# Second feed-forward of a two-layer transformer kernel: up projections by Strassen's scheme, the down projection as a phase of its own

## The chip, the cores and the metric

The kernel runs on one core of a Trainium2 chip. The core has a matrix engine (TensorE, PE in the profile, with its weight loads listed apart as PEld), a vector engine (VectorE, DVE), a scalar engine (ScalarE, ACT), GpSimd (POOL) and a sync engine (SP). SP, ACT and POOL issue DMA transfers between memory (DRAM) and the on-chip memory (SBUF); PE writes its sums to PSUM, from where DVE and ACT read them. The metric is the device time of one execution in microseconds (us).

## The reference, cut to what matters

Two layers on 1024 tokens (and, in layer 0 only, 256 context tokens) of width 1024, all in 32-bit floats. Each layer has a mixer (layer 0 attention, layer 1 a gated linear attention, GLA) and a feed-forward part with a convolution over three tokens. The change concerns the feed-forward part of layer 1 and the final norm behind it.

```python
def conv_ffn(x, w_up, conv_w, conv_b, w_down):      # x: 1024 x 1024, w_up: 1024 x 5632, w_down: 2816 x 1024
    h = x @ w_up
    ch = h.shape[-1]
    h = lax.conv_general_dilated(h, conv_w[:, None, :], window_strides=(1,),
                                 padding=((1, 1),), feature_group_count=ch, ...) + conv_b
    u, gt = jnp.split(h, 2, axis=-1)
    return (jax.nn.silu(gt) * u) @ w_down
...
        h = h + g1 * y
        h = h + g2 * conv_ffn(rms_norm(h, norm2_g[layer]) * (1.0 + sc2) + sh2, ffn_w_up[layer],
                              ffn_conv_w[layer], ffn_conv_b[layer], ffn_w_down[layer])
...
    return rms_norm(h, final_norm_g)
```

## The kernel before

All activations lie transposed: h is eight tiles of 128 channels by 1024 tokens (h0 to h7 in the rows, as hh0 to hh7). A product of 32-bit floats is made of three matmuls: each operand is split into a high part, rounded to the type that PE multiplies (fp32r), and a low part, the rest, and wh·xh, wh·xl and wl·xh are added up in PSUM. `split` (L92 casts on ACT, L72 subtracts on DVE) makes the two parts. `load_w` brings 128 x 1024 weights (512 KB) on SP's queue into `wraw`, which has two buffers, and splits them into `whi` and `wlo`, three buffers each. `proj` (the matmuls of L109) runs one such tile against 1024 channels of the activation, 24 matmuls of 512 tokens. PSUM has two tiles `big` of three banks of 512 and two tiles `sm` of one.

The end of the kernel, in program order: `out_pass` twice (the output projection of GLA, first for tokens 0 to 511, then for 512 to 1023, tile names gA and gB), each of eight steps that add a projection to a row of h. In the second call the norm of tokens 0 to 511 (`norm_mod`, through `rstd_rows`) is made beside the projections after its step 1. `rstd_rows` squares the rows of h on ACT, adds them on DVE into `acc`, sums over channels with one matmul with ones (L127), and takes the inverse root as `yr` on ACT and DVE; `norm_mod` then makes `nu` (scaled rows) and x4h and x4l (the split operand), two DVE rows for each of eight channel blocks.

Then `ffn` runs for the 22 chunks c of 128 hidden channels. Each chunk has two parts, u (column block c of the up weights) and the gate (block c + 22): 48 matmuls of 512 tokens each into a `big`, then the convolution, one ACT row and two DVE rows (scalar_tensor_tensor of 1023, L69) straight from PSUM into `cv`. ACT's silu and one DVE product make the gated product, which is split into gh and gl. After every second chunk `down` runs the down projection of the two finished chunks: eight output blocks by two token halves, six matmuls each into an `sm` (L887), and DVE adds each into h. At the end the last three chunks are finished by token ranges (0 to 511, then 512 to 767 and 768 to 1023, matmuls of 256), and each finished range is normed by `final`, which stores the output by turns on SP's and ACT's queue.

PE's order is written out by hand (`manual_schedule`) from the second `out_pass` to the first projections of `ffn`; elsewhere a scheduler orders each engine's queue by priority and readiness, and the tiles' buffers decide what waits for what.

## Time and profile before

| | us |
|---|---|
| median of 3 runs (lowest to highest) | 3166.31 (3165.25 to 3168.08) |
| profiled execution, its own time | 3165.92 |
| its span, first to last instruction | 3164.1 |
| PE busy in the span | 3048.6 (96%) |
| DVE busy | 2026.3 (64%) |
| ACT busy | 1142.1 (36%) |
| POOL busy | 29.9 (1%) |
| mean granted TensorE clock | 0.987 |

The page gives each engine's busy time, the groups of instructions by line with the mean time of one, and what ended the idle time before them. Matmuls are pipelined: a matmul's recorded duration covers part of its neighbours', so how many fit in a stretch is read from the distance of their starts. The granted clock is a share of full speed (2.4 GHz); 0.5 is 1.2 GHz.

### The profile page before, as it was taken

To read this page: it belongs to the slowest core of one execution; us is meant where nothing else is said; L and a number is where in the kernel's file an instruction comes from. 1 tells how busy PE (TensorE), PEld (TensorE's weight loads), DVE (VectorE), ACT (ScalarE), POOL (GpSimd) and SP (SyncE) were. 2 spreads that over 40 slices of the span, in tenths; PEclk is the share of its full clock that TensorE was granted. 3 is DMA by queue.
4 is the path that set the end of the run, shared out by engine and by line. 5 is a ranking of instruction groups with operands and counts; after the bars stand their busy time and mean duration, and the time that the engine had idled before them with its cause. 6 is when DMAs were issued, how large, how long until landed. Compare 5 with 4: busy or idle time off the path is not lost. (4 is left out here: it accounts for less than half of the span.)

```text
span 3164.1 us, 40097 instructions
## 1 busy us (share of the span) xinstructions
PE 3048.6 (96%) x16390; PEld 2570.0 (81%) x16390; DVE 2026.3 (64%) x3124; ACT 1142.1 (36%) x1884; POOL 29.9 (1%) x50
## 2 busy tenths in 40 slices
PE   8788799999999999999999999999999999999998
PEld 4676689998878888888888788888877888888887
DVE  7667688886588555454455697668766554555446
ACT  5110277776342122122122365445444222222223
POOL 0000000000000000000000000000000000000000
PEclk9989899999999999999999999999999999999999
DMA  6665762212435111111111141110141111111111
GB/s 222 176 173 177 193 167 67 61 54 62 159 115 184 42 40 36 38 40 39 36 41 40 47 154 34 37 57 31 41 175 67 47 43 58 47 47 40 60 47 60
DMA packets 139184, 257.46 MB, mean 81 GB/s; under 512 B 22676, under 2 KB 82196, under 8 KB 139000
## 3 DMA queue, kind: packets, MB, share of 16 engines
q1 hardware_dynamic: 122168, 234.67, 22.7%
q0 software_dynamic: 15104, 18.13, 2.5%
q8 instruction: 129, 2.11, 0.3%
q10 hardware_dynamic: 1728, 2.10, 0.2%
q14 instruction: 55, 0.45, 0.0%
...
## 5 line engine op out<-in xcount | busy, mean ns | idle before, releaser
L92 ACT CAST whi<-wraw 128x1024 fp32r<-128x1024 f32 x218 | 226.2, 1048 | 1120.4 <-PE big L109 638.5
L72 DVE TENSOR_TENSOR wlo<-wraw,whi 128x1024 fp32r<-128x1024 f32 x218 | 264.4, 1221 | 483.0 <-ACT whi L92 481.4
L109 PE MATMUL big<-x2h,whi 128*128 128x512 f32 (+1 forms) x1056 | 377.5, 358 | 1.8 <-ACT crow L75 1.2
L109 PE MATMUL big<-x2l,whi 128*128 128x512 f32 (+1 forms) x1056 | 377.1, 357 | 0.4 <-DVE x2l L69 0.3
L109 PE MATMUL big<-x2h,wlo 128*128 128x512 f32 (+1 forms) x1056 | 377.2, 357 | 0.0
L887 PE MATMUL sm<-gh,whi 128*128 128x512 f32 (+1 forms) x904 | 332.6, 368 | 2.5 <-DVE h L69 1.4
L887 PE MATMUL sm<-gl,whi 128*128 128x512 f32 (+1 forms) x904 | 329.3, 364 | 0.2 <-DVE gl L72 0.2
L887 PE MATMUL sm<-gh,wlo 128*128 128x512 f32 (+1 forms) x904 | 328.7, 364 | 0.0
L69 DVE SCALAR_TENSOR_TENSOR cv<-big,cw,cv 128x1023 f32<-128x1023 f32 (+1 forms) x264 | 267.2, 1012 | 21.0 <-ACT cv L75 17.7
L109 PE MATMUL big<-x4l,whi 128*128 128x512 f32 x704 | 277.8, 395 | 0.9 <-DVE x4l L69 0.9
L109 PE MATMUL big<-x4h,whi 128*128 128x512 f32 x704 | 276.7, 393 | 1.9 <-ACT x4h L75 1.9
L109 PE MATMUL big<-x4h,wlo 128*128 128x512 f32 x704 | 274.0, 389 | 0.0
L69 DVE SCALAR_TENSOR_TENSOR h<-sm,G,h 128x512 f32<-128x512 f32 (+1 forms) x280 | 179.8, 656 | 90.6 <-PE sm L887 89.8
L109 PEld LDWEIGHTS big<-x2h,whi 128*128 128x128 f32 x1056 | 198.8, 188 | 34.1 <-ACT crow L75 2.0
L109 PEld LDWEIGHTS big<-x2l,whi 128*128 128x128 f32 x1056 | 198.8, 188 | 32.5 <-DVE x2l L69 1.1
L109 PEld LDWEIGHTS big<-x2h,wlo 128*128 128x128 f32 x1056 | 198.6, 188 | 31.1
L887 PEld LDWEIGHTS sm<-gh,whi 128*128 128x128 f32 x904 | 170.3, 188 | 41.1 <-DVE h L69 6.9
L69 DVE SCALAR_TENSOR_TENSOR hh<-sm,G,hh 128x512 f32<-128x512 f32 (+1 forms) x192 | 137.5, 726 | 87.5 <-PE sm L887 87.2
L887 PEld LDWEIGHTS sm<-gh,wlo 128*128 128x128 f32 x904 | 170.4, 188 | 27.6 <-issue 0.2
L887 PEld LDWEIGHTS sm<-gl,whi 128*128 128x128 f32 x904 | 170.4, 189 | 26.6 <-DVE gl L72 0.6
L75 ACT ACTIVATE cv<-big,cb,cw 128x1024 f32<-128x1024 f32 (+1 forms) x132 | 130.6, 990 | 125.0 <-DVE cv L69 124.5
L109 PEld LDWEIGHTS big<-x4h,whi 128*128 128x128 f32 x704 | 132.2, 188 | 34.1 <-ACT x4h L75 3.2
...
## 6 DMA issues: line engine op xcount, KB each, us to landing
mraw<-in_mod_wt_dram SPq DMA_DIRECT2D x88, 512.0 KB, 3.8
wraw<-in_ffn_up_dram SPq DMA_DIRECT2D x88, 512.0 KB, 3.2
wraw<-in_ffn_down_dram SPq DMA_DIRECT2D x44, 512.0 KB, 3.2
...
wraw<-in_attn_w_out_dram SPq DMA_DIRECT2D x16, 512.0 KB, 3.8
wraw<-in_gla_w_v_dram SPq DMA_DIRECT2D x16, 512.0 KB, 3.2
wraw<-in_gla_w_out_dram SPq DMA_DIRECT2D x16, 512.0 KB, 3.3
```

Of the source, the lines that this page charges most:

```text
L69: return self.nc.vector.scalar_tensor_tensor(out=out, in0=in0, scalar=scalar, in1=in1, op0=op0, op1=op1)
L72: return self.nc.vector.tensor_tensor(out=out, in0=a, in1=b, op=op)
L75: return self.nc.scalar.activation(out=out, in_=in_, func=func, **kw)
L92: self.nc.scalar.copy(hi, src)
L109: self.nc.tensor.matmul(ps[:, t0:t0 + n], a[:, k, :], b(k, t0, n), start=(k == 0 and j == 0), stop=(k == KD - 1 and j == 2))
L887: nc.tensor.matmul(o, w[:, d * P:(d + 1) * P], x[:, t0:t0 + n], start=(i == 0), stop=(i == 3 * len(group) - 1))
```

## The change

In layer 1 `ffn` is replaced. Layer 0 keeps it.

The up projections of a pair (u and the gate of chunk c) form one product of a 256 x 1024 and a 1024 x 1024 matrix. It is cut into 2 x 2 blocks: the weights into A11, A12, A21 and A22 (128 x 512 each, 1 for u, 2 for the gate, the second digit the half of the channels), the activation into B11, B12, B21 and B22 (512 channels by 512 tokens). Winograd's form of Strassen's scheme takes seven block products P1 to P7 instead of eight, each of 12 matmuls (four channel blocks by three parts): P1 = A11·B11, P2 = A12·B21, P3 = S4·B22, P4 = A22·T4, P5 = S1·T1, P6 = S2·T2, P7 = S3·T3. S1 to S4 are sums and differences of weight blocks, made on DVE for each pair; T1 to T4 are those of the activation, made once by `forms_last`, in place in h. Partial results are added on DVE from PSUM into rooms of 128 x 1024, from which the convolution now reads.

Since h's tiles serve as rooms, h goes to DRAM in both calls of `out_pass` (`spill`, on POOL's queue). Each gated product is stored to DRAM (`gs`, 512 KB, on POOL's queue). Behind the 22 pairs `down_pass` runs three times, for tokens 0 to 511, 512 to 767 and 768 to 1023. Each pass loads and splits all 22 down weights and the gated products of its tokens (`dx`), holds all eight output blocks in PSUM over the 22 chunks, and adds them into h once at its end. h is loaded back within the first pass, and the final norms of the first two ranges stand within the third. PE's order is written out by hand to the end.

In the whole kernel weights are now split in two halves of 512 (`split_half`, one set of 12 buffers of 512 for high and low parts).

```diff
     def load_w(self, src):
-        raw = self.wp.tile([P, 1024], F32, name="wraw", tag="wraw", bufs=2)
+        raw = self.raw_w()
         self.dma(raw, src)
-        hi = self.wp.tile([P, 1024], F32R, name="whi", tag="whi", bufs=3)
-        lo = self.wp.tile([P, 1024], F32R, name="wlo", tag="wlo", bufs=3)
-        self.split(hi, lo, raw, self.urgent)
+        return tuple(zip(*(self.split_half(raw[:, c:c + 512], self.urgent) for c in (0, 512))))
+
+    def raw_w(self):
+        return self.wp.tile([P, 1024], F32, name="wraw", tag="wraw", bufs=2)
+
+    def split_half(self, a, urgent=False):
+        hi, lo = (self.wp.tile([P, 512], F32R, name=n, tag="wf", bufs=12) for n in ("wh", "wl"))
+        self.split(hi, lo, a, urgent)
         return hi, lo
...
+                    if spill:
+                        self.dma2(self.h2[n][t0 // 512], h[n][:, t0:t0 + c])
...
+    def forms_last(self, h, X, A, B):
+
+        y = self.rstd_rows(lambda k, a, b: h[k][:, a:a + b], 512, 512)
+        k4 = range(4)
+        u11, u12, u21, u22 = ([h[k + j][:, t:t + 512] for k in k4] for j, t in ((0, 0), (0, 512), (4, 0), (4, 512)))
+        b1, b2 = ([B[:, k + j:k + j + 1] for k in k4] for j in (0, 4))
+        for k in k4:
+            self.stt(u12[k], u12[k], A[:, k:k + 1], y, ALU.mult, ALU.mult)
+            self.tt(u12[k], u12[k], u11[k], ALU.subtract)
+            self.split(*X["T1"][k], u12[k])
+        for k in k4:
+            hi, lo = X["B22"][k]
+            self.stt(u22[k], u22[k], A[:, k + 4:k + 5], y, ALU.mult, ALU.mult)
+            self.act(hi, u22[k], AF.Identity, bias=b2[k])
+            self.stt(lo, u22[k], b2[k], hi.bitcast(F32), ALU.add, ALU.subtract)
+        for k in k4:
+            self.stt(u22[k], u22[k], b2[k], u12[k], ALU.add, ALU.subtract)
+            self.split(*X["T2"][k], u22[k])
+        for k in k4:
+            self.stt(u11[k], u22[k], b1[k], u11[k], ALU.subtract, ALU.subtract)
+            self.split(*X["T3"][k], u11[k])
+        for k in k4:
+            self.stt(u21[k], u21[k], b2[k], u22[k], ALU.add, ALU.subtract)
+            self.split(*X["T4"][k], u21[k])
...
+    def pair_forms(self, l, c, w, fw, order):
+
+        rg = fw.tile([P, 1024], F32, name="graw", tag="graw", bufs=1)
+        self.dma(rg, self.io["ffn_up"][l, c + NFF])
+        ru = w["raw"]
+        S = {"A11": ru[:, :512], "A12": ru[:, 512:], "A21": rg[:, :512], "A22": rg[:, 512:]}
+
+        def get(n):
+            if n not in S:
+                x, y, op = {"S1": ("A21", "A22", ALU.add), "S2": ("S1", "A11", ALU.subtract), "S3": ("A11", "A21", ALU.subtract),
+                            "S4": ("A12", "S2", ALU.subtract)}[n]
+                x, y = get(x), get(y)
+                S[n] = fw.tile([P, 512], F32, name="S", tag="S", bufs=3)
+                self.tt(S[n], x, y, op)
+            return S[n]
+        for p in order:
+            w[p] = self.split_half(get({1: "A11", 2: "A12", 3: "S4", 4: "A22", 5: "S1", 6: "S2", 7: "S3"}[p]))
...
+            q.order = (5, 3, 6, 7, 4) if c < 2 else (1, 5, 6, 7, 2, 3, 4)
...
+        def prod(q, p):
+            if p == 1:
+                q.big, q.b = self.big(), self.sm()
+                q.a, q.cc, q.d = (q.big[:, 512 * i:512 * i + 512] for i in range(3))
+            ps, start = {1: (q.a, True), 2: (q.a, False), 5: (q.cc, True), 3: (q.cc, False), 6: (q.b, True), 7: (q.d, True), 4: (q.d, False)}[p]
+            (wh, wl), x = q.w[p], X[self.OPERAND[p]]
+            for k in range(4):
+                s = slice(k * P, (k + 1) * P)
+                for j, (a, b) in enumerate(((wh, x[k][0]), (wh, x[k][1]), (wl, x[k][0]))):
+                    nc.tensor.matmul(ps, a[:, s], b, start=(start and k == 0 and j == 0), stop=(k == 3 and j == 2), skip_group_check=True)
...
+            u, e = room[q.c % 2], q.c % 2
+            with self.tc.high_priority():
+                if p == 1:
+                    q.p1 = fw.tile([P, 512], F32, name="p1", tag="p1", bufs=2)
+                    nc.scalar.copy(q.p1, q.a)
+                elif p == 2:
+                    nc.scalar.copy(u[:, :512], q.a)
+                elif p == 5:
+                    q.p5 = half(5, e)
+                    nc.scalar.copy(q.p5, q.cc)
+                elif p == 6:
+                    q.u2 = half(6, e)
+                    self.tt(q.u2, q.b, q.p1, ALU.add)
+                    self.tt(q.p5, q.p5, q.u2, ALU.add)
+                elif p == 7:
+                    self.tt(room[2][:, 512:], q.d, q.p5, ALU.add)
+                elif p == 4:
+                    self.tt(room[2][:, :512], q.d, q.u2, ALU.add)
+                if p == 3:
+                    q.has12 = True
+                if q.u2 is not None and q.has12:
+                    self.tt(u[:, 512:], q.cc, q.u2, ALU.add)
+                    q.has12 = False
...
+        def end(q):
+            cv = []
+            for part, x in ((0, room[q.c % 2]), (1, room[2])):
+                j = q.c + NFF * part
+                y = room[3 + part]
+                cw = self.cw[:, j, :]
+                self.act(y, x, AF.Identity, scale=cw[:, 1:2], bias=self.cb[:, j:j + 1])
+                self.stt(y[:, 1:], x[:, :NM - 1], cw[:, 0:1], y[:, 1:], ALU.mult, ALU.add)
+                self.stt(y[:, :NM - 1], x[:, 1:], cw[:, 2:3], y[:, :NM - 1], ALU.mult, ALU.add)
+                cv.append(y)
+            self.last = self.act(cv[1], cv[1], AF.Silu)
+            self.tt(cv[0], cv[0], cv[1], ALU.mult)
+            self.dma2(self.gs[q.c], cv[0])
+
+        q = begin(0)
+        prod(q, 1)
+        done(q, 1)
+        prod(q, 2)
+        nxt = begin(1)
+        prod(nxt, 1)
+        done(nxt, 1)
+        prod(nxt, 2)
+        self.pair_forms(l, 0, q.w, fw, q.order)
+        last_forms()
+        done(q, 2)
+        for c in range(NFF):
+            for p in q.order:
+                prod(q, p)
+                done(q, p)
+            if c == 0:
+                self.pair_forms(l, 1, nxt.w, fw, nxt.order)
+                done(nxt, 2)
+            else:
+                nxt = begin(c + 1) if c + 1 < NFF else None
+            end(q)
+            q = nxt
...
+    def down_pass(self, l, h, t0, n, dp, mid={}):
+
+        nc = self.nc
+        g = self.G[l][1][:, :, 0]
+        per = 512 // n
+        tiles = [self.big() for _ in range(2 if n == 512 else 1)]
+        banks = [t[:, 512 * i:512 * i + 512] for t in tiles for i in range(3)]
+        banks += [self.sm() for _ in range(2 if n == 512 else 1)]
+        ps = [banks[d // per][:, n * (d % per):n * (d % per) + n] for d in range(KD)]
+        for c in range(NFF):
+            w = self.load_w(self.io["ffn_down"][l, c])
+            x = dp.tile([P, 512], F32, name="dx", tag="dx", bufs=4)[:, :n]
+            self.dma(x, self.gs[c][:, t0:t0 + n])
+            xh = dp.tile([P, 512], F32R, name="dh", tag="dh", bufs=4)[:, :n]
+            xl = dp.tile([P, 512], F32R, name="dl", tag="dl", bufs=4)[:, :n]
+            self.split(xh, xl, x)
+            for d in range(KD):
+                for j, (a, b) in enumerate(((w[0], xh), (w[0], xl), (w[1], xh))):
+                    nc.tensor.matmul(ps[d], self.columns(a, d * P, P), b, start=(c == 0 and j == 0 and d % per == 0),
+                                     stop=(c == NFF - 1 and j == 2), skip_group_check=True)
+            if c in mid:
+                mid[c]()
+        with self.tc.high_priority():
+            for d in range(KD):
+                o = h[d][:, t0:t0 + n]
+                self.stt(o, ps[d], g[:, d:d + 1], o, ALU.mult, ALU.add)
...
+        self.out_pass(io["gla_w_out"], ((MAIN1, oB),), h, self.G[1][0], spill=True, meanwhile={1: lambda: self.forms_first(h, X, A, B)})
...
+        self.ffn_halves(1, fw, h, X, lambda: self.forms_last(h, X, A, B))
...
+        self.down_pass(1, h, 0, 512, dp, {2 + i * KD + k: rows(i, k) for i in range(2) for k in range(KD)})
+        self.down_pass(1, h, 512, 256, dp)
+        self.down_pass(1, h, 768, 256, dp, {2: lambda: final(0, 512), 10: lambda: final(512, 256)})
+        final(768, 256, True)
```

The first place is PE's queue around the ones matmul (`onesm`) of the second norm. Before, it stands between the eighth channel block of the u projection of chunk 0 and the gate projection:

```order
L109 MATMUL big_19737<-x4h7_19380,whi_19724 128x512
L109 MATMUL big_19737<-x4l7_19388,whi_19724 128x512
L109 MATMUL big_19737<-x4h7_19380,wlo_19725 128x512
L127 MATMUL sm_19763<-acc_19766,onesm_80 128x512 [waits DVE_49,PE_49]
L109 MATMUL big_19738<-x4h0_19373,whi_19730 128x512 [waits Activation_49]
L109 MATMUL big_19738<-x4l0_19381,whi_19730 128x512
```

Now the end of P2 of the second pair (big_20478) stands ahead of it, and T1 behind it:

```order
L1070 MATMUL big_20478<-B21h3_20013,wh_20474 128x512
L1070 MATMUL big_20478<-B21l3_20014,wh_20474 128x512
L1070 MATMUL big_20478<-B21h3_20013,wl_20475 128x512
L140 MATMUL sm_20536<-acc_20539,onesm_80 128x512 [waits DVE_49,PE_49]
L1070 MATMUL big_20440<-T1h0_20380,wh_20510 128x512 [waits Activation_49]
L1070 MATMUL big_20440<-T1l0_20381,wh_20510 128x512 [waits DVE_49]
L1070 MATMUL big_20440<-T1h0_20380,wl_20511 128x512
L1070 MATMUL big_20440<-T1h1_20382,wh_20510 128x512
L1070 MATMUL big_20440<-T1l1_20383,wh_20510 128x512 [waits DVE_49]
```

P1 and P2 of two pairs, 48 matmuls, are now issued before the ones matmul, where 24 of chunk 0's u projection were, and the next matmul needs T1, the first of the forms that depend on this norm.

The second place is DVE's queue behind that norm's `yr`. Before, two rows for each channel block, beginning with these:

```order
L69 SCALAR_TENSOR_TENSOR nu_19797<-hh0_18903,A11_86,yr_19790 128x512 [waits DVE_49]
L69 SCALAR_TENSOR_TENSOR nu_19801<-hh1_18904,A11_86,yr_19790 128x512
L69 SCALAR_TENSOR_TENSOR x4l0_19381<-nu_19797,B11_90,x4h0_19373 128x512 [waits Activation_49]
L69 SCALAR_TENSOR_TENSOR x4l1_19382<-nu_19801,B11_90,x4h1_19374 128x512 [waits Activation_49]
L69 SCALAR_TENSOR_TENSOR nu_19805<-hh2_18905,A11_86,yr_19790 128x512 [waits DVE_49]
L69 SCALAR_TENSOR_TENSOR nu_19809<-hh3_18906,A11_86,yr_19790 128x512 [waits DVE_49]
```

Now the first of 44 rows that make T1, B22, T2, T3 and T4 in place:

```order
L69 SCALAR_TENSOR_TENSOR hh0_19489<-hh0_19489,A11_86,yr_20563 128x512 [waits DMASW0_49,DVE_49]
L69 SCALAR_TENSOR_TENSOR hh1_19490<-hh1_19490,A11_86,yr_20563 128x512 [waits DMASW1_49]
L72 TENSOR_TENSOR hh0_19489<-hh0_19489 128x512 [waits DVE_49]
L72 TENSOR_TENSOR hh1_19490<-hh1_19490 128x512 [waits DVE_49]
L69 SCALAR_TENSOR_TENSOR hh2_19491<-hh2_19491,A11_86,yr_20563 128x512 [waits DMASW2_49]
L72 TENSOR_TENSOR T1l0_20381<-hh0_19489,T1h0_20380 128x512 [waits Activation_49]
L72 TENSOR_TENSOR T1l1_20383<-hh1_19490,T1h1_20382 128x512 [waits Activation_49]
L72 TENSOR_TENSOR hh2_19491<-hh2_19491 128x512 [waits DVE_49]
L69 SCALAR_TENSOR_TENSOR hh3_19492<-hh3_19492,A11_86,yr_20563 128x512 [waits DMASW3_49]
L69 SCALAR_TENSOR_TENSOR hh4_19493<-hh4_19493,A11_86,yr_20563 128x512 [waits DMASW4_49]
L72 TENSOR_TENSOR T1l2_20385<-hh2_19491,T1h2_20384 128x512 [waits Activation_49]
```

The next matmul on PE needs T1h0 and T1l0, the third row of each channel block, and the products behind it need forms that stand at the end of these rows.

The third place is DVE's queue in the middle of the stage. Before, for one chunk, the halves of the weights (wlo), the convolution from PSUM and the updates of h:

```order
L72 TENSOR_TENSOR wlo_20130<-wraw_20127,whi_20129 128x1024 [waits DMAHW0_49,PE_49,Activation_49]
L69 SCALAR_TENSOR_TENSOR cv0_19971<-big_19916,cw_19718,cv0_19971 128x1023 [waits Activation_49,Pool_49]
L69 SCALAR_TENSOR_TENSOR cv0_19971<-big_19916,cw_19718,cv0_19971 128x1023 [waits DVE_49]
L69 SCALAR_TENSOR_TENSOR hh0_18903<-sm_20040,G11_94,hh0_18903 128x512 [waits PE_49]
L72 TENSOR_TENSOR wlo_20189<-wraw_20186,whi_20188 128x1024 [waits DMAHW1_49,Activation_49]
L69 SCALAR_TENSOR_TENSOR cv1_20030<-big_19975,cw_19718,cv1_20030 128x1023 [waits Activation_49]
L69 SCALAR_TENSOR_TENSOR hh1_18904<-sm_20045,G11_94,hh1_18904 128x512 [waits PE_49]
L69 SCALAR_TENSOR_TENSOR cv1_20030<-big_19975,cw_19718,cv1_20030 128x1023 [waits DVE_49]
```

Now, for one pair, the stretch from the middle of its products to the middle of the next pair's: hh0 and hh2 are rooms of partial sums, hh3 and hh4 the convolution's, graw and wraw the raw gate and u weights, wl the low halves of weights or weight sums (S), p1 the kept P1.

```order
L72 TENSOR_TENSOR S_21269<-wraw_21239,S_21253 128x512 [waits DVE_49]
L72 TENSOR_TENSOR wl_21262<-S_21259,wh_21261 128x512 [waits PE_49,Activation_49]
L72 TENSOR_TENSOR hh0_19489<-big_21144,hh6_19495 128x512 [waits PE_49,Activation_49]
L72 TENSOR_TENSOR wl_21266<-wraw_21239,wh_21265 128x512 [waits Activation_49]
L69 SCALAR_TENSOR_TENSOR hh3_19492<-hh0_19489,cw_20420,hh3_19492 128x1023 [waits Activation_49]
L69 SCALAR_TENSOR_TENSOR hh3_19492<-hh0_19489,cw_20420,hh3_19492 128x1023 [waits DVE_49]
L72 TENSOR_TENSOR hh2_19491<-big_21144,hh6_19495 128x512 [waits PE_49]
L72 TENSOR_TENSOR wl_21272<-S_21269,wh_21271 128x512 [waits Activation_49]
L69 SCALAR_TENSOR_TENSOR hh4_19493<-hh2_19491,cw_20420,hh4_19493 128x1023 [waits Activation_49]
L72 TENSOR_TENSOR wl_21276<-graw_21241,wh_21275 128x512 [waits PE_49,Activation_49]
L69 SCALAR_TENSOR_TENSOR hh4_19493<-hh2_19491,cw_20420,hh4_19493 128x1023 [waits DVE_49]
```

Rows that read PSUM (`big`, `sm`) and wait for PE now alternate on DVE with weight rows of the next pair, and the updates of h have left this stretch.

## Rows read from the trace of the kernel before

**Rows 1.** The page's head and first part: span, then busy us, share and instructions.
```profile
span 3164.1 us, 40097 instructions
...
PE 3048.6 (96%) x16390; PEld 2570.0 (81%) x16390; DVE 2026.3 (64%) x3124; ACT 1142.1 (36%) x1884; POOL 29.9 (1%) x50
```

**Rows 2.** Windows: from:to, length, PE, PEld, DVE, ACT, POOL busy, clock, DMA share, GB/s.
```profile
2420.00:2440.00 20.00, 17.16 (x68) 11.94 (x67) 15.90 (x22) 9.11 (x12) 0.00 (x0) 1.00 0.07 27
2500.00:2600.00 100.00, 100.00 (x439) 81.99 (x438) 52.46 (x55) 22.32 (x21) 0.00 (x0) 1.00 0.13 43
```

**Rows 3.** Timeline of PE, stage start: start, duration, engine, line, operation, tiles, shape.
```profile
2410.90 0.40 PE L109 MATMUL big<-x4h,whi 128*128 128x512 f32 x1
...
2416.42 1.02 PE L127 MATMUL sm<-acc,onesm 128*128 128x512 f32 x2
```

**Rows 4.** Groups by shape, 2410 to the end: busy us, mean ns, idle before, releaser.
```profile
L109 PE MATMUL big<-x4h,whi 128*128 128x512 f32 x704 | 276.7, 393 | 1.9 <-ACT x4h L75 1.9
...
L69 DVE SCALAR_TENSOR_TENSOR hh<-sm,G,hh 128x512 f32<-128x512 f32 x176 | 130.5, 749 | 83.7 <-PE sm L887 83.5
L887 PE MATMUL sm<-gh,whi 128*128 128x512 f32 x328 | 129.1, 394 | 0.6 <-DVE hh L69 0.5
...
L69 DVE SCALAR_TENSOR_TENSOR cv<-big,cw,cv 128x1023 f32<-128x1023 f32 x88 | 112.5, 1278 | 1.2
L72 DVE TENSOR_TENSOR wlo<-wraw,whi 128x1024 fp32r<-128x1024 f32 x64 | 77.5, 1223 | 205.1 <-ACT whi L92 205.0
...
L92 ACT CAST whi<-wraw 128x1024 fp32r<-128x1024 f32 x64 | 66.2, 1048 | 435.4 <-PE big L109 251.7 <-PE sm L887 183.7
...
L887 PE MATMUL sm<-gh,whi 128*128 128x256 f32 x48 | 14.6, 305 | 0.2 <-DVE hh L69 0.2
```

**Rows 5.** Timeline of PE in the up projections, two matmuls twelve apart.
```profile
2699.28 0.39 PE L109 MATMUL big<-x4l,whi 128*128 128x512 f32 x1
...
2702.03 0.39 PE L109 MATMUL big<-x4l,whi 128*128 128x512 f32 x1
```

**Rows 6.** Timeline of PE in a down projection, two matmuls 28 apart.
```profile
2708.94 0.40 PE L887 MATMUL sm<-gh,whi 128*128 128x512 f32 x1
...
2715.33 0.39 PE L887 MATMUL sm<-gl,whi 128*128 128x512 f32 x1
```

**Rows 7.** Timeline of PE near the end, two matmuls of 256 columns, 14 apart.
```profile
3140.84 0.28 PE L887 MATMUL sm<-gh,whi 128*128 128x256 f32 x1
...
3142.51 0.28 PE L887 MATMUL sm<-gh,wlo 128*128 128x256 f32 x1
```

**Rows 8.** Timeline of PE, the last down matmul.
```profile
3153.05 0.28 PE L887 MATMUL sm<-gh,wlo 128*128 128x256 f32 x1
```

**Rows 9.** Timeline of DVE around the second norm (x2: two rows in one).
```profile
2406.57 1.23 DVE L72 TENSOR_TENSOR wlo<-wraw,whi 128x1024 fp32r<-128x1024 f32 x1
2407.71 0.68 DVE L72 TENSOR_TENSOR acc<-acc,sq 128x512 f32<-128x512 f32 x1
...
2420.88 1.42 DVE L69 SCALAR_TENSOR_TENSOR nu<-hh,A,yr 128x512 f32<-128x512 f32 x2
...
2431.03 1.41 DVE L69 SCALAR_TENSOR_TENSOR x4l<-nu,B,x4h 128x512 fp32r<-128x512 f32 x2
```

**Rows 10.** Timeline of PE early in the kernel, behind an idle stretch (in brackets).
```profile
121.89 0.77 PE L109 MATMUL big<-x1h,whi 128*128 128x512 f32 x1 [8.17 <-DVE slo L72]
122.46 0.63 PE L109 MATMUL big<-x1l,whi 128*128 128x512 f32 x1
...
125.44 0.63 PE L109 MATMUL big<-x1h,wlo 128*128 128x512 f32 x1
```

**Rows 11.** DMA issues, size, median us to landing: whole span, then 2300 to 2410.
```profile
wraw<-in_ffn_down_dram SPq DMA_DIRECT2D x44, 512.0 KB, 3.2
...
wraw<-in_ffn_up_dram SPq DMA_DIRECT2D x4, 512.0 KB, 5.2
```

**Rows 12.** Timeline of DVE in a down projection: a row that waits for PSUM.
```profile
2711.91 0.75 DVE L69 SCALAR_TENSOR_TENSOR hh<-sm,G,hh 128x512 f32<-128x512 f32 x1 [0.63 <-PE sm L887]
```

More of the change, by code (lines that the diff above doesn't have):

```diff
@@ L187, in setup @@
         self.hs = [scratch(f"hs{k}", [P, NM]) for k in range(KD)]
+        self.h2 = [[scratch(f"h2{k}{i}", [P, 512]) for i in range(2)] for k in range(KD)]
+        self.gs = [scratch(f"gs{c}", [P, NM]) for c in range(NFF)]
         self.og = [[scratch(f"og{c}{g}", [P, 512]) for g in range(2)] for c in range(KD)]
@@ L886, in down @@
                             for w, x in ((wh, a), (wh, b), (wl, a)):
-                                nc.tensor.matmul(o, w[:, d * P:(d + 1) * P], x[:, t0:t0 + n],
+                                nc.tensor.matmul(o, self.columns(w, d * P, P), x[:, t0:t0 + n],
                                                  start=(i == 0), stop=(i == 3 * len(group) - 1))
@@ L949, in ffn, with forms, forms_first @@
             after(*t)
+    @staticmethod
+    def forms(pool, names):
+        return {n: [tuple(pool.tile([P, 512], F32R, name=f"{n}{a}{k}") for a in "hl") for k in range(4)] for n in names}
+    def forms_first(self, h, X, A, B):
+        y = self.rstd_rows(lambda k, a, b: h[k][:, a:a + b], 0, 512)
+        for k in range(KD):
+            u = h[k][:, 0:512]
+            hi, lo = X["B11" if k < 4 else "B21"][k % 4]
+            self.stt(u, u, A[:, k:k + 1], y, ALU.mult, ALU.mult)
+            self.act(hi, u, AF.Identity, bias=B[:, k:k + 1])
+            self.stt(lo, u, B[:, k:k + 1], hi.bitcast(F32), ALU.add, ALU.subtract)
@@ new lines, with ffn_halves, begin, done @@
+    OPERAND = {1: "B11", 2: "B21", 3: "B22", 4: "T4", 5: "T1", 6: "T2", 7: "T3"}
+    def ffn_halves(self, l, fw, room, X, last_forms):
+        nc = self.nc
+        half = lambda i, j: room[i][:, 512 * j:512 * j + 512]
+        class Pair:
+            u2 = None
+            has12 = False
+        def begin(c):
+            q = Pair()
+            q.c, q.w = c, {}
+            q.order = (5, 3, 6, 7, 4) if c < 2 else (1, 5, 6, 7, 2, 3, 4)
+            if c < 2:
+                self.pair_first(l, c, q.w)
+            else:
+                q.w["raw"] = ru = self.raw_w()
+                self.dma(ru, self.io["ffn_up"][l, c])
+                self.pair_forms(l, c, q.w, fw, q.order)
+            return q
+        def prod(q, p):
[8 more added lines that the diff above has]
+                    nc.tensor.matmul(ps, a[:, s], b, start=(start and k == 0 and j == 0), stop=(k == 3 and j == 2), skip_group_check=True)
+        def done(q, p):
+            u, e = room[q.c % 2], q.c % 2
[52 more added lines that the diff above has]
+                done(nxt, 2)
+            else:
+                nxt = begin(c + 1) if c + 1 < NFF else None
+            end(q)
+            q = nxt
@@ L1038, in before_last @@
             es_x.close()
-            st["es0"], st["es"], st["es2"] = (self.stack() for _ in range(3))
+            st["es0"], st["esw"], st["es"], st["es2"] = (self.stack() for _ in range(4))
             self.gla_open(st)
@@ L1050, in after_last @@
         def after_last():
-            raw = self.wp.tile([P, 1024], F32, name="wraw", tag="wraw", bufs=2)[:, :KD * 48]
+            raw = self.raw_w()[:, :KD * 48]
             self.dma(raw, io["gla_gate_w1"])
@@ L1054, in after_last @@
             for d in range(2):
-                raw = self.wp.tile([P, 1024], F32, name="wraw", tag="wraw", bufs=2)[:, :512]
+                raw = self.raw_w()[:, :512]
                 nc.gpsimd.memset(raw, 0.0)
@@ L1102, in body @@
             self.o_load(oB, c, self.og[c][1], dma=self.dma2 if c > 5 else None)()
-        self.out_pass(io["gla_w_out"], ((MAIN0, oA),), h, self.G[1][0], first)
+        self.out_pass(io["gla_w_out"], ((MAIN0, oA),), h, self.G[1][0], first, spill=True)
         es_a.close()
         es_x = self.stack()
-        xp = self.pool(es_x, "xn4", side="right")
-        xh = [xp.tile([P, NM], F32R, name=f"x4h{k}") for k in range(KD)]
-        xl = [xp.tile([P, NM], F32R, name=f"x4l{k}") for k in range(KD)]
+        X = self.forms(self.pool(es_x, "xn4", side="right"), ("B11", "B21"))
         self.open_tmp()
+        A, B = self.A[1][1][:, :, 0], self.B[1][1][:, :, 0]
         hsrc = lambda k, a, b: h[k][:, a:a + b]
```

60 lines of the change are left out of this document (42 added, 18 removed).

## The prediction

> **What bounds the kernel now.** I read the page's first part, then the table of windows over the last stage, then the groups of that stage by shape, then timelines of PE and DVE at its start, middle and end. TensorE bounds the kernel: it is busy 96% of the span [rows 1], and in the stage that the change rewrites it is busy for all of a window while DVE works about half and the DMA share is 0.13 [rows 2]. That stage runs from the first x4h matmul at 2410.90 [rows 3] to the end at 3164.1 [rows 1]: 753.2 us.
>
> A busy PE says little about what a matmul costs, because the durations of neighbours overlap (0.39 us each, [rows 4]). The start-to-start spacing counts. In the up projections the two rows of [rows 5] lie twelve matmuls apart: 2.75 / 12 = 0.2292 us. In the down projection 28 steps take 6.39 us, 0.2282 each [rows 6]. With 256 columns 14 steps take 1.67 us, 0.1193 [rows 7]; I use 0.1195, a little more than half of 0.2282. [Rows 4] shows a third of each count, since each product is three matmuls: 3 x 704 = 2112 up, 3 x 328 = 984 down with 512 columns and 3 x 48 = 144 with 256. That is 484.1 + 224.5 + 17.2 = 725.8 us of matmul spacing in 753.2. The other 27.4 us are the tail of 11.0 behind the last matmul at 3153.05 [rows 8] and some 16 us of gaps: at the start, where PE is busy 17.16 of 20 us [rows 2] and waits for x4h, and around the matmuls of the final norm.
>
> **What is removed.** Seven products of 12 matmuls in place of 96 matmuls per pair of chunks: 22 x 84 = 1848, so 264 fewer, 264 x 0.2292 = 60.5 us. All of it is on PE, which is the bound, so it comes off the end unless another engine takes over. The down projection keeps its 24 x 22 x 2 matmuls of 512 as work, but half of them as twice as many of 256: 528 x 0.2282 + 1056 x 0.1195 = 120.5 + 126.2 = 246.7 instead of 241.7, 5.0 us more. PE's matmuls therefore take 423.6 + 246.7 = 670.3 us, 55.5 less than before.
>
> **The new start: +22 us of idle PE.** PE first does P1 and P2 of two pairs (48 matmuls, 11.0 us), then the ones matmul (order rows in the document's section on the change), and then needs T1. Before, the ones matmul at 2416.42 [rows 3] led to the first modulated row at 2420.88 [rows 9], 4.5 us; it now stands behind 11.0 us of matmuls instead of 5.5, and the forms start 16.2 us after the stage does. They are serial on DVE: 12 rows for T1, 8 for B22, 8 each for T2, T3 and T4, 44 in all, 24 scalar_tensor_tensor and 20 tensor_tensor of 512 columns. The sixteen like them before ran from 2420.88 to 2432.4 [rows 9], 0.72 each with their waits for ACT in it. A tensor_tensor of 1024 takes 1.23 but the next starts 1.14 after it [rows 9]: an overlap of 0.09, so one of 512 (0.68) costs about 0.60. Sum 24 x 0.71 + 20 x 0.60 = 29 (32 if each cost 0.72). Pair 0's last product ends behind T4, at 16.2 + 29 + 1.8 = 47 us. PE has 9 products to do by then, 108 x 0.2292 = 24.8 us; 22 us are lost, where before lost about 5 there.
>
> PE's clock may also fall there. In this trace, after 8.17 us without a matmul, spacing was (125.44 - 122.46) / 7 = 0.426 us [rows 10], the lower of its two levels (1.2 GHz). In the new start most matmuls wait for DVE anyway, so only the last dozen or two would be late: 0 to 5 us. The Trainium skill, page "TensorE: Matmul & The Clock Gate", Part 1, states that an idle array is passed only half of its clock pulses, 1.2 GHz; the trace agrees with its 0.426 against 0.229, and by the page the 5 us end is the likelier one.
>
> Pairs 1 to 3 run unevenly: graw has one buffer, the first store of a gated product must land before its room is written again, and silu's table is loaded. No row shows any of this, so I put 6 us for these and the clock, halfway between 0 (the weights split ahead cover it) and 12 (each of three pairs waits one landing, 3.2 us [rows 11], and a clock loss comes on top).
>
> **The steady pair: PE still bounds, with little to spare.** PE needs 84 x 0.2292 = 19.25 us. DVE has 21 rows: 12 of 512 from SBUF (7 weight halves, 4 sums of weight blocks, one sum of partial products) x 0.60 = 7.2; 4 that add a PSUM bank x 0.66 (0.749 less the overlap, [rows 4]) = 2.6; 4 conv rows of 1023 x 1.20 (1.278 less 0.08, [rows 4]) = 4.8; one of 1024 at 1.14: 15.7 us, or 17.5 at full durations [rows 4]. ACT's casts and copies, by the cast's 1.05 us for 1024 [rows 4], come to about 9 us. The four evacuations stand in DVE's one queue, behind each wait the next pair's weights; but these are split some five products (13 us) ahead, so a wait of a microsecond there doesn't reach PE. After pair 0 there are 145 products x 12 x 0.2292 = 398.8 us. The gated product goes out on POOL's queue, which has nothing else in this stage, and 512 KB have about 9 us to land before that room is written again.
>
> **Down projection.** The turn costs about 0.5 us: the first weights were issued before, and one big tile is free. The wide pass is 120.5. In the narrow passes PE takes 24 x 0.1195 = 2.87 us a chunk, and the two wraw buffers must turn round in twice that, 5.74. A turn is landing, ACT's two casts (together 1.05) and the last half's subtraction (0.68): landing plus 1.73. A load of 512 KB lands in 3.2 us [rows 11], which gives 4.93; the 128 KB of dx that go with each are a quarter more bytes, and 3.2 x 1.25 = 4.0 gives 5.73, just what PE needs. So it is covered or nearly: I take +4 us over 44 chunks, for turns that come out 0.2 longer. The upper end is a landing of 5.2, the row of a stretch with much traffic [rows 11]: (6.93 - 5.74) / 2 x 44 = 26 us; the lower end is 0.
>
> Two final norms stand within pass 3 and take ACT and DVE rows and one ones matmul each, with output stores ahead of weight loads on SP's queue: +6 (0 to 10). In the tail, eight rows of h must now be updated behind the last matmul instead of two; [rows 8] had 11.0, I take 13.
>
> **Elsewhere.** All weights are split in two halves of 512, two rows of 0.60 for one of 1.14 [rows 9], and the scheduler orders earlier stages slightly otherwise. PE has 3164.1 - 3048.6 = 115 us without a matmul in the span [rows 1], most of it in those stages, so a shuffle can go either way: 0, with -4 to +6.
>
> **Sum.** 47 + 6 + 398.8 + 0.5 + 120.5 + 126.2 + 4 + 6 + 13 = 722.0 against 753.2: 31.2 less. From the profiled execution, 3165.92 (0.4 below the median, 3166.31), that gives 3134.7, **3135 us**. In other words: 55.5 us of matmuls go, and 24 of them come back as idle PE, 17 at the start.
>
> **Rivals.** (a) *The narrow passes wait for weights.* For: two buffers and 2.87 us a chunk. Against: 3.2 us landing in the steady state. At the upper end above, 26 instead of 4: 3157. (b) *Slower: DVE becomes the bound of the pairs.* If DVE runs at full durations (17.5) and six waits of a pair stay on its path, four for PSUM banks and two for ACT's half of the conv, each like the 0.63 in [rows 12], a pair takes 21.3 instead of 19.25: 21 x 2.05 = 43 us more, 3178. It decides from 20.7 us a pair on. Against it: the overlap of 0.09, and weights split ahead. [...] (c) *The weight forms are late.* graw is reloaded only behind its last use (landing 3.2 to 5.2), and the next pair's sums wait for it in DVE's queue: 1 us a pair, 3156. (d) *All is covered:* no uneven pairs, no weight waits, finals hidden: 16 less, down to 3119.
>
> **Numbers.** Forecast 0.54, (a) 0.15, (b) 0.09, (c) 0.12, (d) 0.10. Measurement tells apart about 0.2%, 6.3 us. Faster by more than that, below 3160: forecast, (c), (d) and half of (a), whose 3157 lies 3 us from that bound, 0.84; (b) 0.09 slower; 0.07 in between. The range runs from (d) to (a) with 6 us of the earlier stages on top: 3118 to 3163.
>
> **What would show it.** Right: 1848 up matmuls at 0.229; PE idle some 22 us between the ones matmul and T4; a pair every 19.3 us with DVE at 80 to 90%; the last pass ending about 13 us after its last matmul. Wrong: pairs of over 20 us with DVE near 100% (b), a PE gap once a pair behind a weight half (c), chunks of over 3.2 us in the 256-column passes (a), or a shift before 2410.

## The result: slower by 3.4%, and where the time went

The changed kernel took 3274.6 us (median of 4 runs, 3271.87 to 3281.52) beside 3167.19 for the kernel before, a ratio of 1.034 with a 95% interval of 1.0325 to 1.0361. The forecast was 3135, 32 us faster; it came out 107 us slower.

The page's head and first part of the changed kernel, which answer to [rows 1]:

```profile
span 3271.6 us, 42233 instructions
...
PE 3024.8 (92%) x16568; PEld 2546.6 (78%) x16568; DVE 2174.4 (66%) x3605; ACT 1316.6 (40%) x2378; POOL 50.6 (2%) x88
```

PE's busy time did fall, by 23.8 us, while the span grew by 107.5: the matmuls were saved and PE waits. The other engines are not full either. Windows of the changed kernel, which answer to [rows 2] (columns as there): the middle of the pairs, then the second and the third down pass.

```profile
2700.00:2800.00 100.00, 84.08 (x348) 63.65 (x346) 65.32 (x86) 37.58 (x53) 2.13 (x4) 1.00 0.18 64
3115.00:3178.00 63.00, 63.00 (x526) 62.92 (x525) 39.75 (x72) 31.69 (x64) 0.00 (x0) 1.00 0.64 203
3179.00:3254.00 75.00, 68.19 (x526) 66.23 (x527) 51.88 (x101) 37.28 (x78) 0.00 (x0) 0.95 0.66 213
```

In the pairs PE is busy 84%, DVE 65%, ACT 38%: no engine is the bound, so a chain through several of them is. The table of PE's waits from 2600 to 2700 us names it (us in total, times, longest):

```profile
PE big L1070 <- DVE hh L72: 8.6, 8, 1.3
PE big L1070 <- ACT hh L1080: 4.8, 5, 1.0
PE big L1070 <- ACT p L1078: 2.7, 4, 0.7
```

All three are not weights but read-outs of PSUM: L1078 and L1080 are ACT's copies of P1 and P2, and the L72 rows into hh are DVE's additions from `big`. PE's timeline over one pair shows four of its seven products beginning late (idle time and releaser in brackets); from the first row to the last is one pair, 2637.43 - 2613.28 = 24.15 us:

```profile
2613.28 0.50 PE L1070 MATMUL big<-T1h,wh 128*128 128x512 f32 x1 [0.68 <-ACT p L1078]
2623.10 0.50 PE L1070 MATMUL big<-B21h,wh 128*128 128x512 f32 x1 [1.29 <-DVE hh L72]
2627.09 0.50 PE L1070 MATMUL big<-B22h,wh 128*128 128x512 f32 x1 [0.96 <-ACT hh L1080]
2630.98 0.50 PE L1070 MATMUL big<-T4h,wh 128*128 128x512 f32 x1 [0.85 <-DVE hh L72]
2637.43 0.50 PE L1070 MATMUL big<-T1h,wh 128*128 128x512 f32 x1 [0.67 <-ACT p L1078]
```

They are P5, P2, P3 and P4, and each follows a product into another bank of the same tile `big`. The read-outs that they wait for are of P1 (bank a), P7 (d), P2 (a) and P3 (cc). Here are those of P1 and P2 in ACT's timeline, then those of P7 and P3 in DVE's, with two other rows ahead of them for DVE's pitch.

```profile
2612.64 0.59 ACT L1078 COPY p<-big 128x512 f32<-128x512 f32 x1
...
2626.46 0.58 ACT L1080 COPY hh<-big 128x512 f32<-128x512 f32 x1
```

```profile
2619.95 0.68 DVE L72 TENSOR_TENSOR S<-graw 128x512 f32<-128x512 f32 x1
2620.55 0.69 DVE L72 TENSOR_TENSOR hh<-hh,hh 128x512 f32<-128x512 f32 x1
...
2622.36 0.69 DVE L72 TENSOR_TENSOR hh<-big,hh 128x512 f32<-128x512 f32 x1
...
2630.23 0.69 DVE L72 TENSOR_TENSOR hh<-big,hh 128x512 f32<-128x512 f32 x1 [2.95 <-PE big L1070]
```

P5 writes cc and starts 0.05 us after the copy of bank a ends (2612.64 + 0.59); P2 writes a and starts just behind the reading of d. None of the four reads a value that the product behind it needs or overwrites.

The same wait is the largest of the start. PE's first matmul of the stage, its first T1 matmul, the copy that this one waits for, and DVE's first two T1 rows (x2):

```profile
2430.39 0.40 PE L1070 MATMUL big<-B11h,wh 128*128 128x512 f32 x1
...
2469.72 0.80 PE L1070 MATMUL big<-T1h,wh 128*128 128x512 f32 x1 [24.81 <-ACT hh L1080]
```

```profile
2469.08 0.58 ACT L1080 COPY hh<-big 128x512 f32<-128x512 f32 x1
```

```profile
2452.40 1.29 DVE L72 TENSOR_TENSOR T1l<-hh,T1h 128x512 fp32r<-128x512 f32 x2
```

T1's first rows were ready at about 2453, but P5 waits until 2469.7 for the copy of P2. That copy goes into h0, a room from which the forms are still read, so it can't come earlier; P5 itself needs nothing of it.

The last feed-forward also began later, at 2430.39 instead of 2410.90 [rows 3]. Stage by stage, in us, against the terms of the prediction:

| | forecast | measured |
|---|---|---|
| begin of the stage, against before | 0 | +19.5 |
| start, to the end of pair 0 | 47 | 62.5 |
| other pairs and turn | 405.3 | 502.7 |
| wide down pass | 120.5 | 119.7 |
| two narrow passes | 136.2 | 139.4 |
| last matmul to the end | 13 | 17.0 |

### The profile page after: what moved, and what is told of

The parts are those of the page before. It is cut to its first block, busy times and chain, and to the rows that moved or that the text cites. A ratio compares the mean times of both kernels' runs of the same rounds, so it can differ in the third digit from the quotient of the medians.

```text
span 3271.6 us, 42233 instructions
## 1 busy us (share of the span) xinstructions
PE 3024.8 (92%) x16568; PEld 2546.6 (78%) x16568; DVE 2174.4 (66%) x3605; ACT 1316.6 (40%) x2378; POOL 50.6 (2%) x88
## 4 chain that ended last, share of the span: by engine, by line
PE 72%; DVE 13%; DMA 6%; ACT 5%; issue 2%; SPq 0%; DVEq 0%; ACTq 0%
PE big L122 30%; PE big L1070 10%; PE sm L903 9%; PE big L1153 4%; DMA mraw<-in_mod_wt_dram 4%; DVE hh L72 2%; PE sm L514 2%; PE big L448 2%; PE sm L563 2%; PE sm L629 2%; PE big L489 2%; PE sm L1556 2%; PE big L497 2%; PE sm L1153 1%; DVE wl L72 1%
## 5 line engine op out<-in xcount | busy, mean ns | idle before, releaser
L92 ACT CAST wh<-wraw 128x512 fp32r<-128x512 f32 x480 | 292.4, 619 | 936.7 <-PE big L122 445.0
L72 DVE TENSOR_TENSOR wl<-wraw,wh 128x512 fp32r<-128x512 f32 x480 | 328.4, 689 | 437.5 <-ACT wh L92 420.7
L122 PE MATMUL big<-x2h,wh 128*128 128x512 f32 (+1 forms) x1056 | 377.6, 358 | 2.4 <-ACT x2h L75 1.3
L122 PE MATMUL big<-x2l,wh 128*128 128x512 f32 (+1 forms) x1056 | 377.3, 357 | 0.4 <-DVE x2l L69 0.3
L122 PE MATMUL big<-x2h,wl 128*128 128x512 f32 (+1 forms) x1056 | 377.1, 357 | 0.0
L122 PEld LDWEIGHTS big<-x2h,wh 128*128 128x128 f32 x1056 | 198.9, 188 | 34.1 <-ACT crow L75 2.0
L122 PEld LDWEIGHTS big<-x2l,wh 128*128 128x128 f32 x1056 | 198.8, 188 | 32.3 <-DVE x2l L69 1.1
L122 PEld LDWEIGHTS big<-x2h,wl 128*128 128x128 f32 x1056 | 198.8, 188 | 30.3
L903 PE MATMUL sm<-gh,wh 128*128 128x512 f32 (+1 forms) x528 | 190.0, 360 | 0.8 <-DVE h L69 0.4
L903 PE MATMUL sm<-gl,wh 128*128 128x512 f32 (+1 forms) x528 | 187.7, 355 | 0.0
```

What stands on the lines that cost most here:

```text
L72: return self.nc.vector.tensor_tensor(out=out, in0=a, in1=b, op=op)
L92: self.nc.scalar.copy(hi, src)
L122: self.nc.tensor.matmul(ps[:, t0:t0 + n], self.columns(a, k * m, m), b(k, t0, n), start=(k == 0 and j == 0), stop=(k == KD - 1 and j == 2))
L903: nc.tensor.matmul(o, self.columns(w, d * P, P), x[:, t0:t0 + n], start=(i == 0), stop=(i == 3 * len(group) - 1))
```

## The experiments

**Theory.** PE waits for the tile, not for the bank: a matmul into one bank of `big` is held until the last reader of any other bank of that tile is done. The waits stand in the program, in the order of PE's instructions (Activation is ACT). Here are the first matmuls of P2, P3 and P4 of one pair in the changed kernel:

```
L1070 MATMUL big_21000<-B21h0_20007,wh_20977 128x512 [waits DVE_49]
L1070 MATMUL big_21000<-B22h0_20396,wh_20983 128x512 [waits Activation_49]
L1070 MATMUL big_21000<-T4h0_20412,wh_20987 128x512 [waits DVE_49]
```

**Rival.** The read-outs truly hold up what follows, through rooms, weights or DVE's queue. **A second theory** is for the late begin: it comes from splitting all weights in halves, which the scheduler turns into another order early in the kernel.

### Each sum in a PSUM tile of its own (own_banks)

```diff
-                q.big, q.b = self.big(), self.sm()
-                q.a, q.cc, q.d = (q.big[:, 512 * i:512 * i + 512] for i in range(3))
+                q.b = self.sm()
+                q.a, q.cc, q.d = (self.ps.tile([P, 512], F32, name=n, tag=n, bufs=2) for n in ("qa", "qc", "qd"))
```

(with a PSUM pool of its own for this stage: six banks in three tags, and two sm).

> Edit: the three sums of a pair (a, cc, d) get three PSUM tiles of one bank each instead of the three banks of one tile big. Theory (the wait is for the tile, not for the bank): in the changed kernel a product starts late whenever another bank of its tile is still being read out, four times a pair; with own tiles these four waits go, a pair takes 19.3 us instead of 24.15, the first T1 matmul no longer waits 24.8 us for the copy of P2 and the stage's start is some 15 us shorter: 3274 - 4.9 x 21 - 15 = 3156 us. Rival (the read-outs really hold up the next product, through rooms, weights or DVE's queue): pairs stay at 24 us, 3274 us. In between, pairs of 20 to 22 us would say that DVE's queue is the next limit.

Measured: 3170.7 us (10 runs), ratio 1.001 (0.9998 to 1.0024). A pair takes 19.23 us, and from 2600 to 2700 PE has no wait at all. The window of that stretch:

```profile
2600.00:2700.00 100.00, 100.00 (x439) 82.05 (x438) 82.70 (x110) 48.81 (x68) 2.66 (x5) 1.00 0.23 84
```

PE is full, and DVE does its work of a pair in 83% of the time. So rooms, weights and DVE's queue hold up nothing in the steady state: 104 us went with the tiles alone, 100 of them in the pairs behind pair 0 and the turn (502.7 to 402.5). The start is left 2 us shorter, not 15: T1 now waits for ACT's cast only, but the next product meets a wait that had been hidden behind the first.

```profile
2450.46 0.79 PE L1071 MATMUL qc<-T1h,wh 128*128 128x512 f32 x1 [7.02 <-ACT T1h L92]
...
2474.90 0.79 PE L1071 MATMUL qc<-B22h,wh 128*128 128x512 f32 x1 [16.34 <-ACT hh L1084]
```

P3 adds to the bank that P5 left, so it must wait for the copy of P5 (L1084), and that copy goes into h5, which the forms read until T4. This one is a true dependence.

### Two sums in one tile, the third alone (shared_ac)

```diff
-                q.a, q.cc, q.d = (self.ps.tile([P, 512], F32, name=n, tag=n, bufs=2) for n in ("qa", "qc", "qd"))
+                q.ac, q.d = (self.ps.tile([P, w], F32, name=n, tag=n, bufs=2) for n, w in (("qac", 1024), ("qd", 512)))
+                q.a, q.cc = q.ac[:, :512], q.ac[:, 512:]
```

> Edit: as own_banks, but a and cc share one tile of two banks; only d has its own. Theory (tile): of the four late products of a pair two remain, P5 (behind the copy of P1, 0.8 us late) and P3 (behind the copy of P2, 1.2 us late), and the long wait of the first T1 product for the copy of P2 remains: pairs of 21.3 us, about 3274 - 2.8 x 21 = 3215 us. Rival (the read-outs really hold up the next product): 24 us a pair, 3274 us. If only the shape of the pool mattered, it would be as fast as own_banks.

Measured: 3220.3 us (2 runs), pairs of 21.72 us (21.3 expected). PE's waits from 2600 to 2700 are the two that were named, five of one and four of the other:

```profile
PE qac L1072 <- ACT hh L1082: 4.8, 5, 1.0
PE qac L1072 <- ACT p L1080: 3.9, 4, 1.0
```

The waits of P2 and P4, whose predecessors now lie in another tile, are gone; those of P5 and P3 are left. The price follows the tiles product by product, which the rival doesn't explain.

### Whole weight tiles again (whole_w)

```diff
-        return tuple(zip(*(self.split_half(raw[:, c:c + 512], self.urgent) for c in (0, 512))))
+        hi = self.wp.tile([P, 1024], F32R, name="whi", tag="whi", bufs=3)
+        lo = self.wp.tile([P, 1024], F32R, name="wlo", tag="wlo", bufs=3)
+        self.split(hi, lo, raw, self.urgent)
+        return hi, lo
...
-        hi, lo = (self.wp.tile([P, 512], F32R, name=n, tag="wf", bufs=12) for n in ("wh", "wl"))
+        self.turn = not getattr(self, "turn", False)
+        n = "whi" if self.turn else "wlo"
+        w = self.wp.tile([P, 1024], F32R, name=n, tag=n, bufs=3)
+        hi, lo = w[:, :512], w[:, 512:]
```

(in `load_w`, then in `split_half`, which now only the pairs use: the two halves of a weight share one tile, taken from the two sets by turns.)

> Edit: load_w splits a whole weight tile of 1024 again (one cast, one subtraction, whi and wlo with three buffers each), as before the change; only the products of the pairs use halves. The rest as changed. Theory (the split in halves, with the order that the scheduler makes of it, delays the first 430 us and a few places behind): the last feed-forward starts at 2411 to 2415 us instead of 2430.4, total 3274 - 17 = 3257 us. Rival (the shift comes from other edits, the spill or the pools): start still at 2430, 3274 us.

Measured: 3243.5 us (4 runs), 31 us less, of which the stage's begin accounts for 15:

```profile
2415.61 0.40 PE L1076 MATMUL big<-B11h,whi 128*128 128x512 f32 x1
```

The second theory holds. The rest was not expected: pairs went from 24.15 to 23.28 us although they run the same work. The waits of P2, P3 and P4 each got a little shorter (now 0.78, 0.68 and 0.78); the products' weights lie in other buffers here and the two readers' queues are ordered otherwise. Which of the two does it was not followed further, since the waits go away with the tiles.

### The halves alone, in the kernel before (before_halves)

The reverse of the last edit, made to the kernel before and nothing else.

> Edit: the kernel before, with only the weight split changed: two halves of 512 in one set of 12 buffers instead of whole tiles. Theory (the halves alone delay the first 430 us and a few places behind): the last feed-forward starts 12 to 20 us later than 2410.9, total 3167 + 15 = 3182 us; the last feed-forward itself takes 753 us as before. Rival (the shift needs the other edits, for instance the pools): 3167 us.

Measured: 3184.7 us (4 runs), ratio 1.005 (1.0036 to 1.0066), 15 us slower. The last feed-forward begins at 2432.73 in its profile, 21.8 us later than before where 12 to 20 were expected (the profiled execution was the slowest of the four, 4 us above their median), and takes 754.2 us, as before.

```profile
2432.73 0.40 PE L118 MATMUL big<-x4h,wh 128*128 128x512 f32 x1
```

Where the halves cost it is seen on SP's queue around 360 us, just ahead of the attention: in the kernel before, in the changed kernel, and in before_halves. A row's second number is how long the queue was held by what it merges.

```profile
360.82 0.33 SPq L78 DMA_DIRECT2D wraw<-in_attn_w_out_dram  x1
...
369.32 0.33 SPq L78 DMA_DIRECT2D am<-in_amask_dram  x1
369.77 4.91 SPq L78 DMA_DIRECT2D kc<-ks  x10
```

```profile
359.11 23.37 SPq L78 DMA_DIRECT2D wraw<-in_attn_w_out_dram  x2
382.66 0.33 SPq L78 DMA_DIRECT2D am<-in_amask_dram  x1
383.40 4.61 SPq L78 DMA_DIRECT2D kc<-ks  x10
```

```profile
360.94 24.26 SPq L78 DMA_DIRECT2D wraw<-in_attn_w_out_dram  x2
385.38 0.33 SPq L78 DMA_DIRECT2D am<-in_amask_dram  x1
```

With halves, one more load of attn_w_out stands ahead of the attention's mask, keys and queries, and waits at the head of SP's queue for its buffer. The mask, keys and queries come 13 to 16 us later. No engine has more work to speak of; a load that isn't needed yet was put in front. That the halves cost the 15 us is shown by this run and whole_w; that it is this one load is read from the rows, and no run moved it alone.

### Own tiles and whole weights together (banks_whole, banks_whole_2)

> Edit: own_banks and whole_w together. Both theories: start at 2411 to 2415, pairs of 19.3 us, 3156 - 17 = 3139 us. If only the tile theory holds: 3156. If neither: 3274.

Measured: 3155.8 us (5 runs), ratio 0.9956 (0.994 to 0.9971). It is 0.4% faster than the kernel before, little, but clear of its interval. The stage begins at 2408.91 and pairs take 19.23 us, as expected. Of the 17 us that are missing most are in the start, which takes 59.6 us where 47.5 were counted on. Its wait is that of own_banks:

```profile
2408.91 0.47 PE L1077 MATMUL qa<-B11h,whi 128*128 128x512 f32 x1 [0.94 <-DVE hh L69]
...
2454.35 0.80 PE L1077 MATMUL qc<-B22h,wlo 128*128 128x512 f32 x1 [16.70 <-ACT hh L1090]
```

> Edit: none, banks_whole again, beside spread_final and with more rounds, since it stands 0.4% from the kernel before. 3156 us is expected, 0.994 to 0.997 of before.

Measured: 3155.75 us (7 runs), ratio 0.9968 (0.9957 to 0.9979). Its profile has the stage begin 6.4 us later, at 2415.3, with the same program: the stages early in the kernel differ by that much from one execution to the next.

### The copy of P5 in a buffer of its own (own_p5)

```diff
-                    q.p5 = half(5, e)
+                    q.p5 = fw.tile([P, 512], F32, name="p5", tag="p5", bufs=2)
```

> Edit: banks_whole, and the copy of P5 goes into a buffer of its own instead of a half of h5. Theory (at the start P3 of pair 0 waits for the copy of P5, which waits until the forms have read h5, 24 us after P5 began): P3 starts as soon as B22 is there, pair 0 ends 7 to 10 us earlier, 3156 - 9 = 3147 us; the steady pairs stay at 19.23. Rival (the forms on DVE are what pair 0 waits for anyway, T4 being the last of them): its end moves by less than 3 us, 3154 us.

Measured: 3156.1 us (4 runs), no gain. P3 did come 16 us earlier, counted from the stage's begin (2411.43 here), but P4, the last product, now has the wait:

```profile
2440.94 0.52 PE L1077 MATMUL qc<-B22h,wlo 128*128 128x512 f32 x1 [0.68 <-ACT p L1090]
...
2462.74 0.76 PE L1077 MATMUL qd<-T4h,whi 128*128 128x512 f32 x1 [6.91 <-DVE hh L72]
```

P4 adds to the bank of P7, whose read-out stands in DVE's queue behind the rows of T4. From the stage's begin to the end of pair 0 it is 56.6 us where banks_whole has 59.6: 3.0 earlier, just beyond the rival's bound and far from the theory's 7 to 10. P4 itself began 5.4 us earlier, but behind its wait of 6.9 us its matmuls started 0.43 us apart at a granted clock of 0.50, where banks_whole has 0.229 at 1.00, and that took back 2.4. The rival was right in the main: the 44 rows on DVE set the start, and freeing one product moves the wait to the next.

### The final norms elsewhere (p5_final2, spread_final)

p5_final2 moves the norm of tokens 0 to 511 from the third pass into the second:

```diff
-        self.down_pass(1, h, 512, 256, dp)
-        self.down_pass(1, h, 768, 256, dp, {2: lambda: final(0, 512), 10: lambda: final(512, 256)})
+        self.down_pass(1, h, 512, 256, dp, {6: lambda: final(0, 512)})
+        self.down_pass(1, h, 768, 256, dp, {6: lambda: final(512, 256)})
```

> Edit: own_p5, and the final norm of tokens 0 to 511 stands in the second down pass (behind its seventh chunk), that of 512 to 767 behind the seventh chunk of the third. Theory (one norm's eight rows of 0.7 us on DVE hold up the weight halves wherever it stands, since the narrow passes have nothing to spare): the waits move to the second pass, total within 3 us of own_p5, 3147. Rival (the two norms crowd each other in the third pass): some 6 us less, 3141 us.

Measured: 3158.1 us (6 runs), 2 us from own_p5. The wait moved along: PE's waits in the second pass, then in the third.

```profile
PE big L1160 <- DVE wlo L72: 3.2, 1, 3.2
```

```profile
PE big L1160 <- DVE wlo L72: 4.9, 4, 2.3
PE big L1160 <- ACT whi L92: 0.5, 1, 0.5
```

spread_final leaves the norms in the third pass of banks_whole, but writes their output rows one per chunk:

```diff
+        mid = {1: lambda: final(0, 512)}
+        for k in range(KD):
+            mid[6 + k] = lambda k=k: out_row(0, 512, k)
+            mid[14 + k] = lambda k=k: out_row(512, 256, k)
+        mid[9] = lambda: (out_row(0, 512, 3), final(512, 256))
```

(out_row is the body of final's loop; final only makes the inverse root.)

> Edit: banks_whole, and in the third down pass the eight output rows of a final norm are written into the program one per chunk instead of all at once. Theory (PE's waits in the third pass, 14.6 us over 22 chunks, come from the eight output rows that DVE runs in a row, 5.4 us, ahead of a weight's low half): with them spread the third pass has 4 to 8 us of waits, total 8 us less than banks_whole, 3148 us. Rival (loads and squares of the norms, or SP's queue, hold the pass up): waits stay at 12 to 15 us, 3156 us.

Measured: 3152.5 us (6 runs), ratio 0.9957 (0.9944 to 0.9969), the fastest, though only 3 us below banks_whole beside it, which its spread (3145 to 3159) doesn't tell apart. The third pass itself went from 77.9 to 72.7 us (79.5 in banks_whole_2). PE's waits there, of banks_whole and then of spread_final:

```profile
PE big L1160 <- DVE wlo L72: 7.9, 4, 4.3
PE big L1160 <- ACT whi L92: 0.3, 1, 0.3
```

```profile
PE big L1160 <- DVE wlo L72: 3.7, 6, 0.8
PE big L1160 <- ACT whi L92: 1.9, 2, 1.2
```

The one long wait for a low half, 4.3 us behind eight rows in a row, is gone; short ones stay. The 14.6 us that the expectation called waits are what the pass has above 22 chunks of 2.88; the tables have 8.2 us of waits before and 5.6 after. So 2.6 of the 5.2 us came from the waits. PE's granted clock differs as well, as the windows of the two passes show (columns as in [rows 2]): 0.93 in banks_whole, 1.00 in spread_final.

```profile
3053.86:3131.78 77.92, 69.97 (x532) 68.31 (x532) 50.51 (x80) 33.75 (x56) 0.00 (x0) 0.93 0.62 203
3057.94:3130.68 72.74, 67.06 (x534) 64.58 (x532) 49.97 (x80) 33.64 (x56) 0.00 (x0) 1.00 0.67 220
```

What the clock is worth in the other 2.6 us, and whether the short waits that stay come from the norms' work or their traffic, was not taken apart.

## Why the prediction was wrong, step by step

**The steady pair.** This is the step that failed. The prediction counted the read-outs as DVE's and ACT's work, asked whether it fits into 19.25 us, and found that "a wait of a microsecond there doesn't reach PE". It looked at what stands behind a read-out on DVE's queue and never at whether PE waits for the read-out itself. It does, four times a pair, because the three sums share one tile: a pair took 24.15 us instead of 19.25, and own_banks gave the difference back (19.23). Rival (b) did name four waits for PSUM banks a pair, at 0.63 us each, but as time that DVE stands still on top of its full durations, and gave that 0.09; the waits were PE's, 0.7 to 1.3 us each, with DVE 65% busy. Rival (c) had weights late, and none of the waits from 2600 to 2700 is for a weight. DVE's count was good: 15.7 us were worked out for a pair, and own_banks has 82.70% of 19.23, 15.9. The page "VectorE: DVE Perf Modes" of the Trainium skill, section "The DRAIN you can't avoid", has the next operation wait until the pipe is empty, but adds that one which is not held starts earlier. Here operations recorded at 0.69 us start every 0.60 (2619.95, 2620.55 and on in the changed kernel), so the trace goes with what the page adds. The overlap that the prediction took from rows held.

**The sign of it could be read beforehand.** The first matmul of P2 waits for DVE, as the order above shows (B21h). It can't be waiting for its weight's high half, which ACT casts, nor for its own bank a, which ACT copies: DVE's part is the reading of another bank.

**The start.** "22 us are lost" was 38: 62.5 us in place of 47. The forms began about as forecast, 18.8 us into the stage (16.2 forecast), and ran their 44 rows at the pitch forecast, to 2477.9. What was missing are the waits of products for read-outs, of which the copies go into rooms that the forms still read. The first is the tile's (P5 for the copy of P2, 24.8 us), and so is that of P7 for the reading of P3 (2.6); the others are true ones (P3 for the copy of P5, P4 for the reading of P7). Own tiles alone leave 60 us there, so this is a second, smaller miss of the same kind: a room that is free in the steady state isn't at the start.

**PE's clock.** The prediction gave 0 to 5 us. Behind the wait of 24.8 us the twelve matmuls of P5 took 5.5 us at a granted clock of 0.50, the lower level (1.2 GHz), and started 0.427 us apart. An estimate from these spacings: 12 x (0.427 - 0.229) = 2.4 us for P5, and some 1.2 for the last matmuls of P7, which ran 0.43 apart, so 3.6, inside the forecast range. It is part of the 62.5.

**The down projection.** The wide pass was right (119.7 for 120.5). Of the narrow passes, rival (a) had weights late; the second pass ran its 22 chunks in 63.6 us without a wait, 2.89 a chunk for 2.87, so the 4 us given to late weights were hardly needed. The third, which holds the two norms, took 75.8, 12 more: the 6 us given to them were too few. The tail was 17.0 for 13, and before it was 11.0:

```profile
3254.22 2.44 DVE L69 SCALAR_TENSOR_TENSOR hh<-big,G,hh 128x256 f32<-128x256 f32 x6 [2.70 <-PE big L1153]
3254.62 0.28 PE L1153 MATMUL sm<-dh,wl 128*128 128x256 f32 x1
...
3256.58 0.87 DVE L69 SCALAR_TENSOR_TENSOR hh<-sm,G,hh 128x256 f32<-128x256 f32 x2
...
3258.72 4.31 PE L140 MATMUL big<-sq,onesm 128*128 128x256 f32 x14
...
3263.07 0.38 ACT L75 ACTIVATE yr<-big 128x256 f32<-128x256 f32 x1 [0.88 <-PE big L140]
```

DVE's first update of h comes when the whole last `big` is done (its last matmul starts at 3253.90), so all eight stand behind it. They end 2.8 us behind the last matmul. The larger part follows: the squares and ones matmuls of all eight rows, 5.6 us until `yr`. The prediction added 2 us for the updates and nothing for these sums.

**Elsewhere.** "0, with -4 to +6" was +19.5. The halves were priced as work, 0.06 us per weight, and their order was let pass as a shuffle that goes either way. It was 15 us one way (before_halves). SP's queue shows one load put ahead of others, 13 us of the 19.5 around 360 us; the order of that queue was there to read.

**What was right.** 264 matmuls fewer at 0.229 each, the pitch of DVE's rows, the pair's 19.25 us (19.23 measured once PE is free), the wide and the second pass. With both faults out the kernel takes 3152 to 3156 us, some 10 to 14 below before: of the 32 us forecast, the rest went to the start (13), the third pass and the tail.
